# A two-layer hybrid backbone: loads of the opening in another order, one-stretch inputs for the last layer's FFN, and another order of the mLSTM's small matmuls

## Chip, cores and metric

The kernel runs on one core of a Trainium2 chip. The metric is the device time of one execution in microseconds. TensorE (PE) multiplies, VectorE (DVE), ScalarE (ACT) and GpSimd (POOL) do elementwise work, and SyncE (SP) issues all DMA loads in one queue.

## The reference

512 latent tokens and 256 context tokens of width 1024 pass through two layers. A layer has an adaLN-modulated RMSNorm, one input projection for four head groups (A windowed attention, B dense attention with RMS-normalised and rotated q and k, C a bidirectional mLSTM, D a Mamba-2 scan), an output projection of all four, and a squared-ReLU MLP of width 4096. Only the latent tokens leave the kernel. Cut to what the change touches:

```python
def rmsnorm(x, g):
    y = xf * lax.rsqrt(jnp.mean(xf * xf, axis=-1, keepdims=True) + EPS)
    return y * g
# dense attention (B)
q = apply_axial_rope(rmsnorm(q, g_q), cos, sin) * scale
k = apply_axial_rope(rmsnorm(k, g_k), cos, sin)
# mLSTM (C), one chunk
s = einsum('bthd,bshd->btsh', qc, kc) * w
num = einsum('btsh,bshv->bthv', s, vc) + decay_prior * einsum('bthd,bhvd->bthv', qc, c_mat)
den = s.sum(axis=2) + decay_prior * einsum('bthd,bhd->bth', qc, n_vec)
c_new = carry_decay * c_mat + einsum('bsh,bshv,bshd->bhvd', wk, vc, kc)
# MLP
def sq_relu_ffn(h, w1, w2):
    return jnp.square(jax.nn.relu(h @ w1)) @ w2
```

## The kernel before

Activations lie with features on the partitions and tokens along the free axis: context in columns 0 to 255 (CTX), latent tokens in 256 to 767 (LAT). Every large product is done in three matmuls on split operands: a weight or activation is split into a rounded part (`h`, `wh`) and a remainder (`hl`, `wl`); `wh` by `h`, `wh` by `hl` and `wl` by `h` are added in PSUM. `wload` (L167) loads a weight block, rounds it on ScalarE (`wh`) and takes the difference on VectorE (`wl`). The tile framework settles the order of instructions on each engine from the program's order and the data they need; each engine then works strictly in that order.

**Opening (L125 to L150, L523 to L592).** The input x comes in four loads of 768 KB (`xr`, L133). Between them stand the loads of `cc` (the conditioning vectors), `cst` (identity and masks), and `pcol`, `prow` (column and row tables, L128). ScalarE squares x (`sq`), TensorE sums over features (`mx`), ScalarE copies the sums (`ssr`), and after a transpose VectorE computes the reciprocal root (`rj`). TensorE spreads it to a row in PSUM (`prow_`), ScalarE copies it to SBUF (`rowx`). `cond(q)` calls `ada_first` (L227) twice: it loads two 512 KB blocks of conditioning weights (`adaw`), multiplies them by the conditioning vector (`silw`), and writes scale and shift into `mod`. `stage(q, sl)` (L561) normalises two feature chunks (`xn`, then `h`, `hl`), which are multiplied with the first projection weights (`wopen`).

**Fill.** `Stream` (L399) holds a list of small pieces of projection work; `fill(t)` emits pieces until a credit of about t microseconds is used up, so that TensorE has projections between the steps of a scan or an attention. `g_feat` (L444) is such a piece: one block of 128 output features over 8 chunks of 128 input features. `g_do` wraps a short function as a piece.

**mLSTM (L1179 to L1394).** While it runs, the stream holds the output gate and the keys and queries of group B. After each of those projections `norm_b` squares it (`bsq`), `col_b` (L1148) sums the squares in matmuls of 2 columns against `cst`, `rsq_b` (L1158) takes the root on VectorE, and `apply_k` (L1167) spreads it by transposes of `kR`. The state loop (L1215) multiplies, for two directions, `vw` by `ktok` and adds into `SC`. The chunk loop (L1340) then has per block of 128 tokens: `c_raw` (q by k on 64 rows, `s<-qT,kT`), the decay matrix `MB` (load, masks on GpSimd, exponentials on ScalarE, product with `c_raw` on VectorE), `fill`, `inter` (`s<-SC,qT`, 130 columns), `fill`, `num` (`s<-v,MB`, eight matmuls of 65 columns) and an evacuation on VectorE (`den`, `yc`). `c_raw`, `inter` and `num` share two PSUM buffers (`s2`) in turn.

**FFN of the last layer (L1458 to L1559).** `ffn1(b)` computes one eighth of the hidden layer, `ffn2(b)` its part of the output. The norm's row is not yet in the inputs: `h2` holds x times its scale in two halves of 256 columns, with 2 columns of the shift between them. So a group of the first product has two stretches, 258 and 256 columns (`psegs`, L1459), and the evacuation multiplies by the row (`rowt`), adds the shift's part (`bs`) in the ReLU, squares and splits:

```python
V.tensor_copy(bs, o[:, 0, NX:NE])
tt(rv, pp, rw, ALU.mult)
act(r[:, sl], r[:, sl], AF.Relu, bias=bs[:, v:v + 1])
tt(r[:, sl], r[:, sl], r[:, sl], ALU.mult)
split_act(r[:, sl], ah, al, sl)
```

The kernel's order is `ffn1(0)`, `ffn1(1)`, `ffn2(0)`, `ffn1(2)`, `ffn2(1)` and so on.

## Time and profile before

| what | value |
|---|---|
| median of 3 timed runs | 1825.8 us (1821.95 to 1827.46) |
| profiled execution | 1831.02 us, its span 1829.2 us |
| mean granted TensorE clock | 0.981 |
| DMA | 178.85 MB, mean 98 GB/s |
| 301.7 to 399.4 us, layer 0's mLSTM | PE busy 94.53 of 97.70 us, clock 0.88 |
| 1295.4 to 1364.0 us, layer 1's mLSTM | PE busy 63.09 of 68.60 us, clock 0.95 |
| DVE busy over the span | 1167.8 us (64%) |

In the profile, a group is named by line, engine, operation and by the tiles it writes and reads; PEld is the load of a matmul's weights, which runs beside the matmuls. PEclk is the clock that was granted to TensorE as a share of full speed. In windows of the profile the columns are: the window and its length, then busy time and instructions of PE, PEld, DVE, ACT and POOL, the granted clock, the share of the DMA engines, and GB/s. An fp32 matmul shows as two instructions there.

### The profile page before, as it was taken

The numbers are of one execution on the slowest core, as the hardware profiler recorded it, in microseconds if no ns is written. First come the engines' busy times: TensorE is split into PE (matmuls) and PEld (weight loads), VectorE is DVE, ScalarE is ACT, GpSimd is POOL, SyncE is SP. The second block draws the span as 40 slices with busy tenths as digits, with TensorE's granted clock in tenths as the row PEclk, the third lists the DMA queues.
The fourth block names the chain that finished last, engine by engine and source line by source line (L and its number), as shares of the span: only waits on it lengthen the run. The fifth ranks groups of instructions, "written<-read, shape, count | busy, mean of one in ns | idle before, by whom it ended". The sixth has DMA issues, their size and how long they took to land. (4 is left out here: it accounts for less than half of the span.)

```text
span 1829.2 us, 31114 instructions
## 1 busy us (share of the span) xinstructions
PE 1756.3 (96%) x11754; PEld 1541.2 (84%) x11754; DVE 1167.8 (64%) x2601; ACT 896.5 (49%) x1988; POOL 330.4 (18%) x332
## 2 busy tenths in 40 slices
PE   7999999989999999999999999999989999999997
PEld 4898888878788888888888888888868899999997
DVE  3578564587877466465465576875588865555555
ACT  4655635455666464354354446563466643333334
POOL 1200111220023363142242531012020200000001
PEclk8999999889999999999999999999999999999999
DMA  9323443331023243233343422132212132322231
GB/s 336 89 82 110 147 139 95 91 121 41 24 82 112 96 132 103 95 127 98 99 127 98 139 70 61 47 94 93 70 58 70 35 105 92 93 93 93 94 96 65
DMA packets 97685, 178.85 MB, mean 98 GB/s; under 512 B 10624, under 2 KB 19200, under 8 KB 97536
## 3 DMA queue, kind: packets, MB, share of 16 engines
q1 hardware_dynamic: 97536, 176.88, 30.1%
q8 instruction: 92, 1.51, 0.3%
q14 instruction: 57, 0.47, 0.1%
HBM read 172.51 MB, written 4.33 MB: 97 GB/s over the span
## 5 line engine op out<-in xcount | busy, mean ns | idle before, releaser
L104 ACT ACTIVATE wh<-wraw 128x512 fp32r<-128x512 f32 (+1 forms) x392 | 238.4, 618 | 257.1 <-PE bulk L96 136.4
L107 DVE TENSOR_TENSOR wl<-wraw,wh 128x512 fp32r<-128x512 f32 (+1 forms) x392 | 281.9, 725 | 116.9 <-ACT wh L104 108.6
L96 PE MATMUL s<-h,wh 128*128 128x258 f32 (+2 forms) x1040 | 316.2, 313 | 1.1 <-ACT pr L104 1.1
L96 PE MATMUL s<-hl,wh 128*128 128x258 f32 (+2 forms) x1040 | 306.2, 313 | 0.0
L96 PE MATMUL s<-h,wl 128*128 128x258 f32 (+2 forms) x1040 | 252.5, 313 | 0.0
L96 PE MATMUL bulk<-ah,wh 128*128 128x512 f32 (+1 forms) x576 | 218.0, 378 | 3.9 <-DVE mod L107 3.2
L302 POOL TENSOR_TENSOR acc<-acc,adap 128x512 f32<-128x512 f32 x96 | 143.2, 1496 | 412.1 <-ACT acc L104 390.6
L96 PE MATMUL bulk<-ah,wl 128*128 128x512 f32 (+1 forms) x576 | 216.1, 375 | 0.0
L96 PE MATMUL bulk<-al,wh 128*128 128x512 f32 (+1 forms) x576 | 215.9, 375 | 0.0
L96 PEld LDWEIGHTS s<-h,wh 128*128 128x128 f32 x1040 | 197.0, 189 | 22.4 <-ACT pr L104 1.6
L115 DVE SCALAR_TENSOR_TENSOR x<-bulk,mod,x 128x512 f32<-128x512 f32 (+1 forms) x224 | 149.4, 671 | 103.3 <-PE bulk L96 102.2
L96 PEld LDWEIGHTS s<-hl,wh 128*128 128x128 f32 x1040 | 197.5, 190 | 11.8 <-issue 0.4
L96 PEld LDWEIGHTS s<-h,wl 128*128 128x128 f32 x1040 | 166.1, 190 | 1.1
L96 PE MATMUL bulk<-h,wh 128*128 128x512 f32 (+1 forms) x416 | 154.0, 370 | 3.8 <-DVE VS L107 2.3
L96 PE MATMUL bulk<-hl,wh 128*128 128x512 f32 (+1 forms) x416 | 144.8, 348 | 0.0
L96 PE MATMUL bulk<-h,wl 128*128 128x512 f32 (+1 forms) x416 | 144.5, 347 | 0.0
L96 PEld LDWEIGHTS bulk<-ah,wh 128*128 128x128 f32 x576 | 108.3, 188 | 24.9 <-DVE mod L107 4.9
L96 PEld LDWEIGHTS bulk<-ah,wl 128*128 128x128 f32 x576 | 108.2, 188 | 21.2
L96 PEld LDWEIGHTS bulk<-al,wh 128*128 128x128 f32 x576 | 108.3, 188 | 19.4
L104 ACT ACTIVATE relu<-relu,bs 128x512 f32<-128x512 f32 x96 | 58.8, 644 | 131.1 <-DVE relu L107 131.1
L104 ACT ACTIVATE adap<-adar,silw 128x256 f32<-128x256 f32 x192 | 85.2, 497 | 56.9 <-DMA adar<-in_wada_dram 52.6
L107 DVE TENSOR_TENSOR relu<-relu 128x512 f32<-128x512 f32 x96 | 88.1, 943 | 31.4 <-ACT relu L104 31.3
(357 smaller groups left out, 3767.3 us busy)
## 6 DMA issues: line engine op xcount, KB each, us to landing
wraw<-in_wf_dram SPq DMA_DIRECT2D x256, 256.0 KB, 2.7
adar<-in_wada_dram SPq DMA_DIRECT2D x96, 256.0 KB, 3.0
wraw<-in_win_dram SPq DMA_DIRECT2D x80, 256.0 KB, 2.8
ada<-in_wada_dram SPq DMA_DIRECT2D x64, 256.0 KB, 4.0
adaw<-in_wada_dram SPq DMA_DIRECT2D x16, 512.0 KB, 6.8
wraw<-in_wout_dram SPq DMA_DIRECT2D x32, 256.0 KB, 3.0
x<-in_xin_dram SPq DMA_DIRECT2D x8, 768.0 KB, 5.0
CB<-drows SPq DMA_DIRECT2D x10, 512.0 KB, 7.0
```

The source lines that it names most:

```text
L96: return TE.matmul(o, lhsT=l, rhs=r, start=start, stop=stop)
L104: return S.activation(o, i, f, scale=scale, **kw)
L107: return V.tensor_tensor(o, a, b, op)
L115: return V.scalar_tensor_tensor(o, a, s, b, op0, op1)
L302: G.tensor_tensor(acc[:, v], acc[:, v], dst, ALU.add)
```

## The change

1. Opening: all four loads of x (and `cc`) stand first in SyncE's queue, then `cst` and layer 0's `pcol`, then the first four conditioning loads (`ada_load`), then the first weights (`W0`), and only then both `prow` and layer 1's `pcol`. `stage(0)` reads the norm's row from PSUM (`prows`); the copy to `rowx` comes after it.
2. `g_feat` takes a waiting function from the list `mids` and runs it in the middle of its eight chunks. `later` puts `col_b` and `rsq_b` on that list, so the 2-column matmuls fall inside the next projection.
3. State loop: both directions' `vw` are made first, then one `fill` of double size, then all `ktok` matmuls.
4. Chunk loop: `inter` comes straight after `c_raw`; the fills ahead of `num` are put together, and a share (0.4 of `wb`) is put between the two halves of `num`.
5. Last layer's FFN: `whole()` multiplies x by the row on GpSimd, applies scale and shift on ScalarE and splits the result into 512 adjacent columns of `h2`. The upper 256 columns are written before `ffn1(1)`, the lower 256 (over the old inputs) before `ffn1(2)`. From b = 2 on, a group is one stretch of 512 columns, and its evacuation is ReLU, square and split.

```diff
     for q in range(4):
         SY.dma_start(xr[q], xin[:, 2 * q:2 * q + 2, :])
         if q == 0:
             SY.dma_start(cc, cin)
-        if q == 1:
-            SY.dma_start(cs, cst)
-        if q == 2:
-            load_cols(0)
+    SY.dma_start(cs, cst)
+    SY.dma_start(pcs[0], pcol[0])
...
+            todo = mids.pop(0) if mids else None
             for k in range(len(W)):
+                if todo is not None and k == len(W) // 2:
+                    todo()
...
+            raws0 = [ada_load(i, (4, 0)[i]) for i in range(2)]
...
-            cond(0)
-            load_cols(1)
+            cond(0, raws0)
+            W0 = wload([wopen[i, 0] for i in range(2)])
+            for l_ in range(DEPTH):
+                load_row(l_)
+            SY.dma_start(pcs[1], pcol[1])
...
-                    norm_chunk(xr[c // 2][:, c % 2, sl], sl, s[:, c:c + 1], md[:, i, c:c + 1], rows[i], *hs[c], pool=c % 2 == 1)
+                    norm_chunk(xr[c // 2][:, c % 2, sl], sl, s[:, c:c + 1], md[:, i, c:c + 1], (rows if q else prows)[i], *hs[c], pool=c % 2 == 1)
+                if q == 0:
+                    act(rows[i], prows[i], AF.Copy)
...
+        def later(*fs):
+            return g_do(lambda: mids.append(lambda: [f() for f in fs]), 0.4 * len(fs))
...
+        def cq(m):
+            return later(*[col_b(f"q{m}", sl, sqq) for sl in segs_q], rsq_b(f"q{m}", jq))
+
+        gs = [later(*[col_b("k", sl, sqk) for sl in (LAT, CTX)], rsq_b("k")), gq(0, LAT)]
+        gs += [gq(0, CTX)] if need else []
+        gs += [cq(0), g_do(apply_k(LAT), 0.5), g_do(apply_k(CTX), 0.5), gq(1, LAT)]
...
-                fill(wu * fC_)
+                vws.append(vw)
+            fill(2 * wu * fC_)
+            for d in range(2):
+                j, vw = ORDERS[d][st], vws[d]
...
             raw = c_raw(j)
+            inter = s2()
+            for e in range(2):
+                for q in range(2):
+                    er = slice(64 * e, 64 * e + 64)
+                    mm(inter[:, e, q * 130:(q + 1) * 130], qT[er, q, js], SC[er, :, j, q, :])
...
+            fill((wa + 0.6 * wb) * fC_ if ji < nout - 1 else 1.5 * FILL_CB[l][4])
             num = s2()
             for e in range(2):
+                if e:
+                    fill(0.4 * wb * fC_ if ji < nout - 1 else 0.5 * FILL_CB[l][4])
...
+        def whole():
+            for c in range(8):
+                t = T((P, NL), F32, "ada", 4, "xn") if c % 2 == 0 else ta((P, NL), name="xn")
+                nrm.append(t)
+                G.tensor_tensor(t, xr[c // 2][:, c % 2, LAT], rowt[0], ALU.mult)
+                act(t, t, AF.Identity, scale=sc2[0][:, c:c + 1], bias=md[:, 0, 24 + c:25 + c])
+                put_whole(c, 1)
+
+        def put_whole(c, i):
+            dst = slice(NE + 256 * i, NE + 256 * i + 256)
+            split_act(nrm[c][:, 256 * i:256 * i + 256], h2[c][0][:, dst], h2[c][1][:, dst], slice(0, 256))
...
+                    if full:
+                        act(r[:, LAT], o[:, 0, :], AF.Relu)
+                        tt(r[:, LAT], r[:, LAT], r[:, LAT], ALU.mult)
+                        split_act(r[:, LAT], ah, al, LAT)
+                        continue
```

How the change moves instructions is shown at three places. The first is SyncE's queue at the program's start, before:

```order
L133 DMA x_65<-in_xin_dram 128x1536
L135 DMA cc_64<-in_cin_dram 128x16
L133 DMA x_66<-in_xin_dram 128x1536
L137 DMA cst_63<-in_cst_dram 128x386
L133 DMA x_67<-in_xin_dram 128x1536
L129 DMA pcol_69<-in_pcol_dram 128x102
L130 DMA prow_71<-in_prow_dram 128x40
L133 DMA x_68<-in_xin_dram 128x1536
L232 DMA adaw_189<-in_wada_dram 128x1024
```

The same place after the change:

```order
L132 DMA x_65<-in_xin_dram 128x1536
L134 DMA cc_64<-in_cin_dram 128x16
L132 DMA x_66<-in_xin_dram 128x1536
L132 DMA x_67<-in_xin_dram 128x1536
L132 DMA x_68<-in_xin_dram 128x1536
L135 DMA cst_63<-in_cst_dram 128x386
L136 DMA pcol_69<-in_pcol_dram 128x102
L228 DMA adaw_101<-in_wada_dram 128x1024
```

The last quarter of x (x_68) has moved ahead of `cst`, `pcol` and `prow`, and `prow` is gone from this part of the queue.

The second place is TensorE in layer 0's mLSTM, where the first block's `num` ends and the second block begins (`s_...` are the PSUM tiles of the chunk loop, `bulk_...` those of the projections), before:

```order
L96 MATMUL s_792_4147<-v_576_2808,MB_4061 128x65 x8
L96 MATMUL bulk_4141<-cst_63,bsq_4095 128x2 x4
L96 MATMUL s_797_4172<-qT_3419,kT_3082 128x128 x4
L96 MATMUL bulk_4194<-cst_63,bsq_4130 128x2 x2
L221 MATMUL bulk_4198<-cst_63,adrow_3988 128x128
L96 MATMUL s_804_4222<-SC_3795,qT_3419 128x130 x4
L96 MATMUL s_809_4258<-v_576_2808,MB_4177 128x65 x2
```

After the change, the same 2-column matmuls and what stands around them, one block later:

```order
L96 MATMUL bulk_4217<-h_179,wl_4010 128x512
L96 MATMUL bulk_4235<-cst_63,bsq_4095 128x2 x4
L96 MATMUL bulk_4217<-h_181,wh_4015 128x512
L96 MATMUL bulk_4217<-hl_182,wh_4015 128x512
L96 MATMUL bulk_4241<-cst_63,bsq_4143 128x2 x2
L96 MATMUL bulk_4217<-h_181,wl_4016 128x512
L96 MATMUL s_804_4227<-v_576_2808,MB_4200 128x65 x4
L96 MATMUL s_814_4280<-qT_3419,kT_3082 128x128 x4
L96 MATMUL bulk_4217<-h_183,wh_4015 128x512
L96 MATMUL s_815_4285<-SC_3795,qT_3419 128x130 x4
```

The `bsq` matmuls now lie between 512-column projections, `num` comes in halves of four, and `inter` (SC) follows `c_raw` (qT, kT) closely.

The third place is TensorE a few blocks on, where the keys of group B are scaled (`kR`), before:

```order
L96 MATMUL s_825_4372<-v_576_2808,MB_4288 128x65 x2
L96 MATMUL s_830_4397<-qT_3419,kT_3082 128x128
L1176 MATMUL bulk_4366<-cst_63,kR_4364 128x128 x4
L96 MATMUL s_830_4397<-qT_3419,kT_3082 128x128 x3
L1176 MATMUL bulk_4429<-cst_63,kR_4427 128x128 x2
L96 MATMUL s_839_4440<-SC_3795,qT_3419 128x130
L96 MATMUL bulk_4433<-h_168,wh_4001 128x512
```

After the change:

```order
L96 MATMUL s_820_4345<-v_576_2808,MB_4290 128x65 x4
L96 MATMUL s_826_4379<-qT_3419,kT_3082 128x128 x4
L96 MATMUL s_827_4384<-SC_3795,qT_3419 128x130 x4
L96 MATMUL s_838_4441<-v_576_2808,MB_4389 128x65 x4
L1190 MATMUL bulk_4416<-cst_63,kR_4414 128x128 x4
L96 MATMUL s_838_4441<-v_576_2808,MB_4389 128x65 x4
L1190 MATMUL bulk_4424<-cst_63,kR_4422 128x128 x2
L96 MATMUL bulk_4428<-h_173,wh_4003 128x512
```

Here a whole block (`c_raw`, `inter` and `num`) stands between two projections with no projection matmul inside.

More of the change, by code (lines that the diff above doesn't have):

```diff
@@ L225, in ada_cols, with ada_load, ada_first @@
            pcs[l][:, C_BADA + 2 * cb:C_BADA + 2 * cb + 2].unsqueeze(1).to_broadcast([P, 2, 2]), ALU.add)
-    def ada_first(i, cb):
+    def ada_load(i, cb):
+        raws = []
+        for kh in range(2):
+            raws.append(k6(raw_roles[(2 * i + kh) % 8], (P, 4, 256), name="adaw"))
+            SY.dma_start(raws[kh], wada[0, cb, kh])
+        return raws
+    def ada_first(raws, cb):
         pt_ = mx((P, 256))
@@ L442, in tile_hybrid_backbone @@
     fill = stream.fill
+    mids = []
     def g_feat(m, acts, sl, evac):
@@ L569, in tile_hybrid_backbone @@
                     stage(q, sl)
-                W = wload([wopen[i, q] for i in range(2)])
+                W = wload([wopen[i, q] for i in range(2)]) if q else W0
                 WT, WF = W[:2], W[2:]
@@ L1216, in tile_hybrid_backbone @@
             kv_ = mx((P, 2, 2, 65))
+            vws = []
             for d in range(2):
@@ L1352, in tile_hybrid_backbone @@
             tt(MBe, MBe, raw[:, :, 0:256].unsqueeze(1).to_broadcast([P, 2, 2, 256]), ALU.mult)
-            fill(wa * fC_ if ji < nout - 1 else FILL_CB[l][4])
-            inter = s2()
-            for e in range(2):
-                for q in range(2):
-                    er = slice(64 * e, 64 * e + 64)
-                    mm(inter[:, e, q * 130:(q + 1) * 130], qT[er, q, js], SC[er, :, j, q, :])
-            fill(wb * fC_ if ji < nout - 1 else FILL_CB[l][4])
+            fill((wa + 0.6 * wb) * fC_ if ji < nout - 1 else 1.5 * FILL_CB[l][4])
             num = s2()
             for e in range(2):
+                if e:
+                    fill(0.4 * wb * fC_ if ji < nout - 1 else 0.5 * FILL_CB[l][4])
                 for q in range(2):
@@ L1409, in tile_hybrid_backbone @@
                 [(kv, j) for j in out_tok for kv in range(2)]
+        assert not mids
         head = attend_s("B", *units[0])
@@ L1459, in tile_hybrid_backbone @@
         psegs = [(0, slice(NE, NE + NL)), (1, slice(0, NE))] if need else [(0, slice(0, NE)), (1, slice(NE, NE + 256))]
+        def whole():
[8 more added lines that the diff above has]
+            split_act(nrm[c][:, 256 * i:256 * i + 256], h2[c][0][:, dst], h2[c][1][:, dst], slice(0, 256))
+        nrm = []
         def ffn1(b):
+            full = not need and b >= 2
             rl = AT_ROLES[b % 2]
@@ L1469, in ffn1 @@
                 ks = [(m, [i], k) for i in range(2) for m in range(2) for k in range(8)] if b == 0 else [(m, [0, 1], k) for m in range(2) for k in range(8)]
+                sg = [(0, slice(NE, NE + NL))] if full else psegs
+                if full:
+                    ks = [(m, [0], k) for m in range(2) for k in range(8)]
                 for m, pi, k in ks:
@@ L1476, in ffn1 @@
                     h, lo = W[k]
-                    parts = [(o[:, psegs[i][0], 0:psegs[i][1].stop - psegs[i][1].start], psegs[i][1]) for i in pi]
+                    parts = [(o[:, sg[i][0], 0:sg[i][1].stop - sg[i][1].start], sg[i][1]) for i in pi]
                     for pp, sl in parts:
@@ L1482, in ffn1 @@
                         mm(pp, lo[:, ms], h2[k][0][:, sl], False, k == 7)
-                    if k < 7 or pi[-1] == 0:
+                    if k < 7 or (pi[-1] == 0 and not full):
                         continue
@@ L1553, in tile_hybrid_backbone @@
         for b in range(8):
+            if not need and b == 1:
+                whole()
+            if not need and b == 2:
+                for c in range(8):
+                    put_whole(c, 0)
             at = ffn1(b)
```

31 lines of the change are left out of this document (11 added, 20 removed).

## Prediction

> **What bounds the kernel now.** I read the page first: the share of each engine and the granted clock in 40 slices.
>
> ```profile
> PE 1756.3 (96%) x11754; PEld 1541.2 (84%) x11754; DVE 1167.8 (64%) x2601; ACT 896.5 (49%) x1988; POOL 330.4 (18%) x332
> PEclk8999999889999999999999999999999999999999
> ```
>
> TensorE is busy 96% of the span and everything else has slack, so a time is gained in three ways only: TensorE starts earlier, streams fewer or cheaper columns, or runs less at a lowered clock. The second row says that the clock is lower in two places, the opening and slices 15 and 16 (around 320 to 410 us). Next I read windows of those places, then the timeline inside them, then the stage with the most matmuls, the last layer's FFN.
>
> **The opening.** SyncE issues loads in program order. The rows below are windows of the DMA rate, then the timelines of SyncE, ScalarE, VectorE and TensorE (start, duration, engine, what; in brackets the idle time and its releaser).
>
> ```profile
> 5.00:8.60 3.60, 2.47 (x11) 0.59 (x12) 0.85 (x5) 3.03 (x5) 0.00 (x0) 1.00 1.00 405
> 8.60:11.00 2.40, 2.40 (x12) 0.38 (x8) 0.25 (x2) 1.58 (x3) 0.00 (x0) 1.00 0.51 165
> 15.00:25.00 10.00, 8.19 (x75) 4.59 (x79) 2.25 (x14) 2.58 (x6) 0.00 (x0) 0.66 1.04 403
> ...
> 3.82 0.46 SPq L130 DMA_DIRECT2D prow<-in_prow_dram  x1
> 4.32 0.45 SPq L133 DMA_DIRECT2D x<-in_xin_dram  x1
> ...
> 7.25 1.58 ACT L104 ACTIVATE sq<-x 128x768 f32<-128x768 f32 x2 [0.43 <-DMA x<-in_xin_dram]
> 9.65 1.58 ACT L104 ACTIVATE sq<-x 128x768 f32<-128x768 f32 x2 [0.82 <-DMA x<-in_xin_dram]
> 14.43 1.57 ACT L104 ACTIVATE sq<-x 128x768 f32<-128x768 f32 x2 [1.73 <-DMA x<-in_xin_dram]
> 18.02 0.98 ACT L104 ACTIVATE ssr<-mx 64x512 f32<-64x512 f32 x2 [2.02 <-PE mx L96]
> 24.67 0.87 ACT L104 ACTIVATE rowx<-s 128x512 f32<-128x512 f32 x2 [2.29 <-PE s L96]
> 27.29 0.72 ACT L104 ACTIVATE h<-xn,mod 128x512 fp32r<-128x512 f32 x1 [0.28 <-DVE mod L107]
> ...
> 12.49 0.17 DVE L111 TENSOR_SCALAR nsk<-prow 128x4 f32<-128x4 f32 x1 [2.14 <-DMA prow<-in_prow_dram]
> ...
> 28.06 0.39 PE L96 MATMUL s<-wh,h 128*128 128x256 f32 x1 [1.71 <-ACT h L104]
> ```
>
> The second quarter of x lands at 7.25, the third at 9.65, the fourth only at 14.43: between them the queue works on the column and row tables (prow lands at 12.49) and the DMA rate falls from 405 to 165 GB/s. The sum of squares, the statistics' row and the first real matmul at 28.06 all follow that fourth quarter.
>
> The change loads all of x ahead of the tables. Third quarter: the 193 KB of constants (0.48 us at 405 GB/s) no longer stand before it, 9.65 - 0.48 = 9.2. Fourth: one quarter takes 9.65 - 7.25 - 0.48 = 1.9 us, so it lands at 11.1, **3.3 us earlier**. The rest of the chain (ssr, transposes, VectorE's rsqrt, the row's matmuls) is unchanged and moves with it. What could be late next is the conditioning weights: ahead of the first two stand 0.25 MB of tables (0.6 us), perhaps the slow stretch of 8.60:11.00 again (2.40 x (1 - 165/405) = 1.4 us), and their own 1 MB (2.6 us): 11.1 + 4.6 = 15.7, before their matmuls can start at about 16.8. The first weights follow by about 20 us, and are wanted at about 22. The 0.87 us of rowx goes behind h, but h waits for mod, not for rowx, so I count nothing there. **Opening: -3.2 us**; at least -0.6 (if the slow stretch stays ahead of x and only the constants go), at most -4.5 (with rowx and a clock that stays up).
>
> **The last layer's FFN.** Before, 512 tokens run as two stretches of 258 and 256 columns. I take the rate from VectorE's first evacuation of each group, then look at who could do the new work.
>
> ```profile
> 1526.51 0.68 DVE L107 TENSOR_TENSOR relu<-s,row 128x512 f32<-128x512 f32 x1
> 1543.87 0.68 DVE L107 TENSOR_TENSOR relu<-s,row 128x512 f32<-128x512 f32 x1
> 1571.96 0.68 DVE L107 TENSOR_TENSOR relu<-s,row 128x512 f32<-128x512 f32 x1
> ...
> 1461.00:1800.00 339.00, 339.00 (x2196) 309.50 (x2195) 188.46 (x310) 119.51 (x195) 0.00 (x0) 1.00 0.29 92
> ...
> L302 POOL TENSOR_TENSOR acc<-acc,adap 128x512 f32<-128x512 f32 x96 | 143.2, 1496 | 412.1 <-ACT acc L104 390.6 <-ACT adap L104 18.6
> ...
> 1461.08 0.39 ACT L104 ACTIVATE row<-mx 128x256 f32<-128x256 f32 x1 [4.46 <-PE mx L96]
> 1473.03 0.63 ACT L104 ACTIVATE wh<-wraw 128x512 fp32r<-128x512 f32 x1 [5.74 <-PE s L96]
> ```
>
> TensorE is full throughout at full clock. 1526.51 to 1543.87 is three groups of 48 small matmuls, 5.79 us a group. To 1571.96 comes one more group and a block of the second product, 96 matmuls of 512 columns: 28.09 - 5.79 = 22.30, or 0.232 us each. After the change a group is 24 of those, 5.58 us: 0.21 us less, in 6 blocks x 4 groups: **-5.1 us**. VectorE's product with the row and the shift's columns go too, but beside a full TensorE that is worth nothing.
>
> The price is the new inputs: 8 GpSimd products (1.5 us each by the L302 row, so done 12 us after row, at about 1473.5), then on ScalarE 8 affine steps and 8 casts, on VectorE 8 differences. ScalarE has a hole of 5.74 us ending at 1473.03, and the new steps fill it; but the last two affine steps wait for GpSimd and stand ahead of the weights' cast of 1473.03. That cast comes some 2 us later (1473.5 and the last affine step and casts behind it): +2 if TensorE wants these weights at once, 0 if it is still at work on the block before. I take the middle, **+1.0 us** (0 to +3, which is two GpSimd products). The second half of the inputs is written under the 22.30 us of the second product, which covers 8 casts and 8 differences; uncovered, they would cost at most 8 x 0.63 = 5.0 us, by the cast's row at twice their width. FFN: -4.1.
>
> **The mLSTM's stretch, and the clock.** These windows show where the clock falls, then what TensorE does in one of them, and what VectorE does behind it.
>
> ```profile
> 329.40:332.80 3.40, 3.04 (x32) 2.62 (x31) 3.28 (x11) 0.75 (x2) 1.76 (x2) 1.00 0.50 117
> 332.80:336.20 3.40, 3.40 (x38) 2.62 (x38) 2.18 (x7) 0.98 (x4) 2.04 (x3) 0.50 0.60 202
> 349.90:360.10 10.20, 10.20 (x39) 7.60 (x38) 5.72 (x14) 3.56 (x12) 2.85 (x4) 0.50 0.21 52
> 373.80:384.00 10.20, 9.60 (x58) 7.32 (x58) 8.78 (x31) 6.19 (x13) 1.50 (x1) 0.50 0.79 252
> 1336.30:1339.70 3.40, 3.40 (x10) 2.72 (x10) 2.86 (x9) 1.51 (x4) 1.81 (x2) 0.51 0.00 0
> ...
> 329.19 1.00 PE L96 MATMUL bulk<-cst,bsq 128*128 128x2 f32 x8
> 330.12 0.71 PE L96 MATMUL s<-qT,kT 64*128 64x128 f32 x8
> 330.76 0.61 PE L96 MATMUL bulk<-cst,bsq 128*128 128x2 f32 x4
> 331.23 0.31 PE L221 MATMUL bulk<-cst,adrow 128*128 128x128 f32 x1
> 331.47 0.72 PE L96 MATMUL s<-SC,qT 64*128 64x130 f32 x8
> 332.55 0.63 PE L96 MATMUL s<-v,MB 128*128 128x65 f32 x3 [0.36 <-DVE kck L1155]
> ...
> 341.50 0.68 DVE L107 TENSOR_TENSOR yc<-yc,s 128x512 f32<-128x512 f32 x1
> 342.17 1.21 DVE L107 TENSOR_TENSOR MB<-MB,s 128x1024 f32<-128x1024 f32 x1
> ```
>
> Clock 0.50 starts right behind windows with many small matmuls. In 329.40:332.80 TensorE waits 0.36 us in all, yet streams little: eight matmuls of 2 columns take 1.00 us, where a 512-column one takes 0.23, and the window holds no projection at all. Half clock holds for 3.4, 10.2 and 10.2 us in layer 0 and 3.4 in layer 1, 27.2 us, with TensorE busy in nearly all of it: work of 13.6 us takes 27.2, **13.6 us lost**.
>
> The change moves the 2-column matmuls into the middle of the next projection, splits the 65-column ones (MB) by projection matmuls, and joins the two products on 64 rows. In the new order layer 0's first and last low windows and layer 1's are broken up so. But at the key's rotation (kR) MB, qT, SC, MB and kR now stand in a row with no projection among them: I keep two windows of 3.4 us there. **Clock: -(27.2 - 6.8)/2 = -10.2 us** (0 to -13.6).
>
> The Trainium skill, "TensorE: Matmul & The Clock Gate", section "Why this matters for your kernels", lays the drop to idle gaps over about 3 us between bursts. This trace differs: it drops with a longest gap of 0.36 us. By that rule this term is 0; that is a rival below.
>
> What it adds: SC's product (inter) now follows qT's at once, in a PSUM buffer that the turn before frees with yc (0.68 us) right after its MB matmuls. Behind it in TensorE's queue stand projection matmuls that were ahead of it. With VectorE free, 0.68 + 0.16 - 0.71 of qT is under 0.3 us a turn; with an MB product in front (1.21 us) 1.5. Ten turns at 0.4, and once at kR the whole of yc and MB's product, 1.5: **+5.5 us** (0 to +18.9, which is ten times 0.68 + 1.21).
>
> The state update's matmuls (vw) now run for both directions at once:
>
> ```profile
> 301.46 0.28 PE L96 MATMUL bulk<-wh,hl 128*128 128x256 f32 x1
> 301.68 0.45 PE L96 MATMUL mx<-vw,ktok 128*64 128x65 f32 x8
> 302.06 0.38 PE L96 MATMUL bulk<-wh,h 128*128 128x256 f32 x1
> 302.28 0.28 PE L96 MATMUL bulk<-wl,h 128*128 128x256 f32 x1
> 302.40 0.28 PE L96 MATMUL bulk<-wh,hl 128*128 128x256 f32 x1
> ```
>
> A 256-column matmul starts 0.12 us behind its neighbour, but 0.22 on the way into and out of the small ones: 0.2 us an excursion, and 10 of 20 go: **-2.0** (0 to -2.0). The projection matmuls that stand ahead of each pair cover VectorE's vw; without them a pair would wait for one vw more.
>
> **Sum**: -3.2 - 4.1 - 10.2 + 5.5 - 2.0 = **-14.0 us**. The profiled execution took 1831.0 (span 1829.2 and 1.8 around it): 1817.0. It lies 5.2 over the median of the runs shown, 1825.8, so I forecast **1812.0**.
>
> **Rivals.** (1) *The clock does not follow the small matmuls' places*: the windows stay at half clock, and only the rest counts: -14.0 + 10.2 = -3.8, 1822.0. For it: the time at half clock may come from dependencies that move along. Against: the window ahead of 332.80 held nothing but small matmuls. (2) *All clusters dissolve and VectorE keeps up*: -13.6 for -10.2, +2 for +5.5: -20.9, 1804.9. For it: VectorE is busy 64% of the span only. (3) *Slower: inter's early place stalls TensorE in every turn*, since it stands in order behind yc and MB's product: 10 x 1.89 = +18.9, and these stalls keep the clock where it is: -3.2 - 4.1 - 2.0 + 18.9 = +9.6, 1835.4. It decides from 0.93 us a turn with no gain of clock. Against: no such wait shows before, and there projections stood ahead of inter. (4) *The opening does not do what it says*: the slow stretch comes from the queue and not from prow, -0.6 for -3.2: 1814.4.
>
> The Trainium skill, same page, section "What's actually happening", has a free-running window of 3413 ns. The half-clock stretches of 3.4 and 10.2 us agree: so where windows fall shifts with the opening, and from run to run.
>
> **How the numbers follow.** Forecast 0.43, rival (1) 0.17, (2) 0.24, (3) 0.06, (4) 0.10. Within 0.3% (1820.3 to 1831.3) is what a measurement of this kernel can hardly tell from no change. Faster: nearly all of the forecast and (4), all of (2), a little of (1): 0.76. Same: most of (1) and a tail: 0.17. Slower: (3) and its surroundings, 0.07. Range: from a little under (2) to a little over (1), 1801 to 1824; it leaves out (3) and the ends where all bounds fall together.
>
> **What would show it.** Opening: the fourth sq at about 11.1, the first wh matmul at about 25. FFN: groups of 5.6 us from block 2 on, no product with row there; a gap of 1 us near 1473 (less the gains). Clock: no 0.50 right after the first turn's MB; one stretch of about 7 us at kR. Waits: TensorE idle before SC under 0.5 us a turn. It is wrong if the clock rows look as before, or if SC is released by yc for over a microsecond each time.

## The result and the profile after

The changed kernel takes 1819.0 us (median of 13 runs, 1815.89 to 1821.77). The kernel before, run beside it, takes 1831.33 us (13 runs, 1821.95 to 1836.26). The ratio is 0.994 with a 95% interval of 0.9925 to 0.9955, so the change gains about 12 us. The forecast was 1812.0 us with a range of 1801 to 1824. The profiled execution took 1820.27 us (span 1818.5), 10.7 less than the one of before.

The page of the changed kernel, busy time of TensorE and the granted clock in 40 slices:

```profile
PE   7999999989999999999999999999989999999997
PEclk9999999899999999999999999999989999999999
```

Before, the first slice and the eighth and ninth (320 to 410 us) showed a lower clock (the prediction names the same times, but calls them slices 15 and 16). Now the eighth does, and the thirtieth (1320 to 1365 us) is new: half clock has become less in layer 0 and has not gone. Where the 10.7 us lie is read from five stretches of the trace. Each runs from one matmul that both kernels have to another: the opening ends at the first `KHL` by `EO`; the mLSTM stretch of layer 0 runs from the first transpose of `kT` to the 33rd `yh` by `wh`, that of layer 1 from the 13th transpose of `kT` to the 241st `KHL` by `EO`; "inputs" runs from the 353rd transpose of `pr` to the 289th `bulk` of `ah` by `wh` and holds `whole()`; "FFN" runs on to the 561st. The rest is the span less these five; no edit of this study touches its code.

| us | opening | mLSTM, layer 0 | mLSTM, layer 1 | inputs | FFN | rest | span |
|---|---|---|---|---|---|---|---|
| before | 88.2 | 118.3 | 90.7 | 66.6 | 312.7 | 1152.7 | 1829.2 |
| after | 83.8 | 113.1 | 86.6 | 70.5 | 308.2 | 1156.3 | 1818.5 |
| difference | -4.4 | -5.2 | -4.1 | +3.9 | -4.5 | +3.6 | -10.7 |

**Opening.** Windows of the DMA rate, then rows of ScalarE and TensorE in the changed kernel:

```profile
8.60:11.00 2.40, 2.40 (x15) 0.56 (x12) 0.00 (x0) 1.82 (x3) 0.00 (x0) 1.00 1.02 402
...
11.08 1.58 ACT L104 ACTIVATE sq<-x 128x768 f32<-128x768 f32 x2 [0.35 <-DMA x<-in_xin_dram]
13.80 0.98 ACT L104 ACTIVATE ssr<-mx 64x512 f32<-64x512 f32 x2 [1.15 <-PE mx L96]
23.14 0.39 PE L96 MATMUL s<-wh,h 128*128 128x256 f32 x1 [2.11 <-ACT h L104]
```

The stretch that ran at 165 GB/s runs at 402, and the last quarter of x is squared from 11.08 on (14.43 before). The first real matmul comes at 23.14, 4.9 earlier than before. Of these, 3.35 come from the load; the sums behind it gain 0.9 more (`ssr` 18.02 to 13.80), since the clock was halved from 15.4 to 22.2 us before and stays full here until 24.6; the last 0.7 lie behind them.

**mLSTM.** The layer-0 stretch before:

```profile
295.20:413.50 118.30, 110.60 (x799) 92.94 (x800) 74.44 (x207) 53.10 (x121) 22.70 (x24) 0.87 0.30 94
```

and after, with windows inside it, then rows of the second sum of the key's norm, of the key's rotation (`kR`) and of the second sum of a query's norm, and TensorE's groups of `inter` and of the column sums over the whole run (busy, mean ns, idle before and its releasers):

```profile
291.80:404.90 113.10, 101.94 (x800) 87.80 (x800) 74.07 (x207) 53.25 (x121) 21.17 (x24) 0.92 0.31 98
331.80:335.20 3.40, 2.05 (x15) 1.57 (x15) 1.66 (x6) 2.58 (x9) 0.98 (x2) 1.00 0.43 165
335.20:342.00 6.80, 6.80 (x31) 5.38 (x30) 3.99 (x17) 0.00 (x0) 0.00 (x0) 0.50 0.40 77
348.83:352.24 3.41, 2.96 (x28) 2.79 (x28) 3.09 (x8) 1.36 (x5) 1.12 (x1) 1.00 0.54 142
352.24:355.66 3.42, 3.28 (x18) 2.54 (x16) 1.38 (x6) 2.16 (x7) 1.93 (x3) 1.00 0.01 2
359.10:362.50 3.40, 3.40 (x20) 2.55 (x19) 2.87 (x11) 0.83 (x2) 0.20 (x1) 0.50 0.02 5
...
334.29 0.61 PE L96 MATMUL bulk<-cst,bsq 128*128 128x2 f32 x4 [1.35 <-DVE kck L1169]
350.92 0.61 PE L1190 MATMUL bulk<-cst,kR 128*128 128x128 f32 x4
357.93 0.61 PE L96 MATMUL bulk<-cst,bsq 128*128 128x2 f32 x4 [0.60 <-DVE kcq L1169]
...
L96 PE MATMUL s<-SC,qT 64*128 64x130 f32 x80 | 8.5, 320 | 1.8 <-DVE yc L107 1.1 <-DVE den L115 0.7
L96 PE MATMUL bulk<-cst,bsq 128*128 128x2 f32 x64 | 8.1, 245 | 2.3 <-DVE kck L1169 1.6 <-DVE kcq L1169 0.6
```

TensorE is busy 8.7 us less and idle 3.5 us more (118.30 - 110.60 = 7.7, then 113.10 - 101.94 = 11.2). The mean clock rises from 0.87 to 0.92: half clock holds for 10.2 us between 330 and 390 instead of 23.8 (a further 6.8 us at the end of the stretch stand in both). `inter` waits 1.8 us in ten turns for VectorE. A wait that was not forecast stands beside it: the second column sum of a pair now waits for VectorE's copy (`kck`, `kcq`), because `bulk` has two PSUM buffers, the projection that is interrupted holds one and the first sum the other. Half clock follows the windows with the two longest of these waits: from 335.2 behind the 1.35 us, and from 359.1 behind the 0.60 us at 357.93. It does not follow the key's rotation: the window 348.83:352.24 holds only small matmuls, `kR` among them, and the one behind it stays at 1.00.

**FFN.** ScalarE's first step for one group and for the group after next; then TensorE, VectorE and GpSimd around the new inputs, and the window behind:

```profile
1520.07 0.60 ACT L104 ACTIVATE relu<-s 128x512 f32<-128x512 f32 x1 [5.19 <-PE s L96]
1531.24 0.60 ACT L104 ACTIVATE relu<-s 128x512 f32<-128x512 f32 x1 [3.14 <-PE s L96]
...
1458.50 0.58 PE L96 MATMUL s<-h,wl 128*128 128x258 f32 x1 [2.29 <-DVE wl L107]
...
1455.03 0.68 DVE L107 TENSOR_TENSOR relu<-s,row 128x512 f32<-128x512 f32 x1
1456.69 1.75 DVE L107 TENSOR_TENSOR wl<-wraw,wh 128x512 fp32r<-128x512 f32 x1
...
1451.46 12.69 POOL L1489 TENSOR_TENSOR xn<-x,row 128x512 f32<-128x512 f32 x8 [3.76 <-ACT row L104]
...
1458.20:1461.60 3.40, 3.10 (x14) 3.10 (x15) 3.40 (x4) 0.56 (x2) 3.40 (x3) 0.50 0.25 82
```

A group takes (1531.24 - 1520.07)/2 = 5.58 us, as forecast. But TensorE stands still for 2.29 us at 1456.2 (the forecast had a gap near 1473) for a weight's remainder (`wl`), which took VectorE 1.75 us instead of 0.69, while GpSimd multiplied; and half clock for 3.4 us follows at once, another 1.7 us.

### The profile page after: what moved, and what is told of

Read it like the earlier page. It is cut to its first block, busy times and chain, and to the rows that moved or that the text cites. A ratio compares the mean times of both kernels' runs of the same rounds, so it can differ in the third digit from the quotient of the medians.

```text
span 1818.5 us, 29949 instructions
## 1 busy us (share of the span) xinstructions
PE 1741.9 (96%) x11178; PEld 1508.9 (83%) x11178; DVE 1162.6 (64%) x2569; ACT 904.2 (50%) x2012; POOL 341.1 (19%) x340
## 4 chain that ended last, share of the span: by engine, by line
PE 78%; DVE 7%; ACT 5%; DMA 4%; issue 3%; POOL 3%; SPq 0%; POOLq 0%; ACTq 0%; DVEq 0%
PE bulk L96 38%; PE s L96 29%; PE mx L96 8%; PE mx L740 2%; DMA MB<-drows 1%; DMA CB<-drows 1%; ACT wh L104 1%; DVE wl L107 1%; ACT qs L104 1%; DMA adar<-in_wada_dram 1%; POOL acc L304 1%; DVE x L115 1%; DMA x<-in_xin_dram 0%; ACT pr L104 0%; DVE yc L107 0%
## 5 line engine op out<-in xcount | busy, mean ns | idle before, releaser
L96 PE MATMUL s<-h,wh 128*128 128x512 f32 (+2 forms) x848 | 292.4, 347 | 1.1 <-ACT pr L104 1.1
L96 PE MATMUL s<-hl,wh 128*128 128x512 f32 (+2 forms) x848 | 282.3, 346 | 0.0
L96 PE MATMUL s<-h,wl 128*128 128x512 f32 (+2 forms) x848 | 252.1, 346 | 2.3 <-DVE wl L107 2.3
L96 PEld LDWEIGHTS s<-h,wh 128*128 128x128 f32 x848 | 161.1, 190 | 30.9 <-ACT pr L104 1.6
L96 PEld LDWEIGHTS s<-hl,wh 128*128 128x128 f32 x848 | 161.4, 190 | 19.8 <-issue 0.2
L96 PEld LDWEIGHTS s<-h,wl 128*128 128x128 f32 x848 | 143.7, 190 | 12.2 <-DVE wl L107 2.5
L107 DVE TENSOR_TENSOR relu<-relu 128x512 f32<-128x512 f32 x96 | 89.3, 956 | 66.9 <-ACT relu L104 66.6
L96 PEld LDWEIGHTS bulk<-ah,wh 128*128 128x128 f32 x576 | 108.3, 188 | 24.6 <-DVE mod L107 4.2
L96 PE MATMUL bulk<-wh,h 128*128 128x256 f32 (+1 forms) x304 | 92.5, 304 | 0.7 <-DVE ra L107 0.4
```

What stands on the lines that cost most here:

```text
L96: return TE.matmul(o, lhsT=l, rhs=r, start=start, stop=stop)
L107: return V.tensor_tensor(o, a, b, op)
```

## The experiments

Twelve kernels were run. The table has their ratio to the kernel before, run beside them, and the stretches of their one profiled execution. e_open to e_vw are the kernel before with one part of the change; the others are the changed kernel with one edit, e_both with two.

| kernel | median us | ratio (95%) | opening | mLSTM 0 | mLSTM 1 | inputs | FFN | rest |
|---|---|---|---|---|---|---|---|---|
| e_open | 1826.01 | 0.9973 (0.9961 to 0.9985) | 83.3 | 118.3 | 91.0 | 66.5 | 312.8 | 1151.6 |
| e_ffn | 1831.80 | 0.9997 (0.9979 to 1.0015) | 89.8 | 118.3 | 90.7 | 69.6 | 308.3 | 1154.4 |
| e_mids | 1829.18 | 0.9991 (0.9977 to 1.0004) | 85.8 | 118.1 | 87.0 | 66.6 | 312.7 | 1155.1 |
| e_inter | 1824.81 | 0.9968 (0.9952 to 0.9984) | 90.2 | 111.2 | 88.1 | 66.6 | 312.8 | 1153.5 |
| e_vw | 1826.73 | 0.9978 (0.9965 to 0.9991) | 85.6 | 110.9 | 88.6 | 66.6 | 312.8 | 1153.6 |
| e_onesum | 1814.40 | 0.9905 (0.9887 to 0.9923) | 83.8 | 111.2 | 85.4 | 70.7 | 308.2 | 1153.7 |
| e_wholevec | 1816.78 | 0.9918 (0.9903 to 0.9934) | 84.7 | 111.2 | 90.3 | 66.7 | 308.2 | 1154.3 |
| e_wholelate | 1816.93 | 0.9916 (0.9900 to 0.9933) | 84.8 | 112.4 | 88.4 | 69.4 | 308.2 | 1151.8 |
| e_nomids | 1813.77 | 0.9909 (0.9892 to 0.9926) | 84.1 | 107.9 | 87.8 | 70.6 | 308.2 | 1152.2 |
| e_interback | 1818.98 | 0.9936 (0.9920 to 0.9952) | 83.9 | 114.0 | 85.7 | 70.6 | 308.2 | 1155.2 |
| e_prowthird | 1818.64 | 0.9931 (0.9911 to 0.9952) | 84.5 | 110.7 | 88.4 | 70.6 | 308.2 | 1152.4 |
| e_both | 1808.19 | 0.9877 (0.9857 to 0.9898) | 83.8 | 109.1 | 85.0 | 66.7 | 308.2 | 1152.3 |

How far a stretch varies without any edit is read from the same table: the unchanged opening lies between 85.6 and 90.2 in five profiles, the changed one between 83.3 and 84.8 in nine; the rest between 1151.6 and 1156.3 in all fourteen, the highest of them in the changed kernel's own profile. The mLSTM stretches of the unchanged code lie at 118.3 and 90.7 to 91.0 in three profiles, those of the changed code at 110.7 to 113.1 and 86.6 to 90.3 in four. So one profile of an edited mLSTM says little about a difference of 2 or 3 us, and ratios that differ by 0.2% have overlapping intervals.

### e_open: the opening alone

```diff
+    SY.dma_start(cs, cst)
+    SY.dma_start(pcs[0], pcol[0])
...
+            W0 = wload([wopen[i, 0] for i in range(2)])
+            for l_ in range(DEPTH):
+                load_row(l_)
```

> The kernel before with the opening's part alone (all of x first, first conditioning weights next, tables later, row read from PSUM). Theory A (the parts add up; x's fourth quarter was held up by the tables): fourth square of x at about 11.1 us, first wh matmul at about 23.1, every later stage 4.3 us earlier than before as the profile of the full change has it at 84 us; time -4 us. Theory B (only the constants' 0.5 us were in x's way, the rest of the gain in the full change comes from elsewhere): -0.6 us, fourth square not before 13.8.

The opening takes 83.3 us and the kernel 0.27% less, about 5 us: theory A. The fourth square starts at 12.03, not at 11.1, because in this execution the second quarter was late already (8.21 instead of 7.27); the quarters follow each other in 1.9 us, as in the changed kernel. No half clock falls into this opening.

### e_ffn: the new inputs alone

```diff
+            full = not need and b >= 2
...
+            if not need and b == 1:
+                whole()
```

> The kernel before with the one-stretch inputs of the last layer's FFN alone. Theory A (the prediction: groups 0.21 us cheaper, 24 of them, less 1.0 for a weight cast that waits): -4.1 us. Theory B (from the profile of the full change: while GpSimd forms its 8 products, VectorE's tensor_tensor takes 1.7 instead of 0.7 us, a weight's remainder comes late, TensorE waits about 2.3 us and may lose another 1.7 at half clock): groups -4.5, price +2.3 to +4: -0.5 to -2.2 us.

The FFN stretch is 4.4 shorter and the stretch of the inputs 3.0 longer; the time is the same as before (0.9997). Theory B: this part gains next to nothing as it stands.

### e_mids: the column sums alone

```diff
+                if todo is not None and k == len(W) // 2:
+                    todo()
```

> The kernel before with the column sums of the q and k norms moved into the middle of the next projection, and nothing else. Theory A (the clock falls behind windows that stream little, and clusters of small matmuls make such windows): half clock in layer 0's mLSTM (23.8 us before between 330 and 385) falls to about 10 us, and 6 us are gained there, less what the sums wait for in their new place: two bulk PSUM buffers, one of them held by the open projection, so the second sum waits for VectorE's copy (kck) of the first, 1.35 and 0.6 us in the full change; net -3 to -5 us in layer 0. Theory B (the clock follows something else, the sums' place does not matter): 20 us or more at half clock remain, net 0 to +2.

Layer 0's stretch is 0.2 us shorter. Half clock holds there for 20.4 us (338 to 348, 379 to 389), and TensorE waits 1.95 us for `kck` at 337.19. That is theory B for layer 0; in layer 1 the stretch is 3.7 shorter. The kernel gains 0.09%, not told from nothing.

### e_inter: the chunk loop alone

```diff
+            inter = s2()
...
+            fill((wa + 0.6 * wb) * fC_ if ji < nout - 1 else 1.5 * FILL_CB[l][4])
```

> The kernel before with the chunk loop's part alone (inter right behind c_raw, fills joined, a share of the fill between the halves of num). Theory A (the full change's profile: inter waits for VectorE's den and yc 0.2 to 0.9 us in some turns, 1.8 us in layer 0 and 1.6 with what stands beside it in layer 1; the split num breaks one cluster): waits of 2 to 4 us added, half clock in layer 0's mLSTM down by one stretch of 3.4 to 6.8 us: -1 to +2 us net. Theory B (the prediction's size): +5.5 of waits, with the clock where it was: +5 us.

The best single part: 7.1 us in layer 0, 2.6 in layer 1, 0.32% of the time. Neither theory had this size. No wait ahead of `inter` is above 0.3 us in either stretch, and two of the three half-clock stretches of layer 0 are shorter or gone (335 to 339 and 356 to 363 are left). The second of these follows the key's rotation, which stands in the first of two windows here:

```profile
352.30:355.70 3.40, 3.29 (x30) 2.82 (x29) 2.59 (x8) 1.81 (x7) 1.27 (x1) 1.00 0.56 133
355.70:359.10 3.40, 3.40 (x18) 3.30 (x18) 1.34 (x7) 2.22 (x6) 1.92 (x3) 0.50 0.08 24
```

TensorE waits 0.11 us in that window (3.40 - 3.29), which holds small matmuls alone.

### e_vw: the state loop's pairs alone

```diff
+            fill(2 * wu * fC_)
+            for d in range(2):
+                j, vw = ORDERS[d][st], vws[d]
```

> The kernel before with the state loop's pairs alone (both vw first, one fill of double size, then all ktok matmuls). Layer 0's mLSTM stretch, from the first transpose of kT to the 33rd yh by wh matmul, took 118.30 us before, 111.24 with the chunk loop's part alone, 113.07 in the full change. Theory A (the prediction: 10 of 20 excursions of 0.2 us go): -1 us in layer 0, -1 us in layer 1, time -2. Theory B (the pairs cost something that explains why the full change gains less there than the chunk loop alone): +0.5 to +2 us in layer 0, time 0 to +2.

From the first transpose of `kT` to the first `inter`, with the same matmuls in between (268 records in both), layer 0 takes 26.39 us instead of 27.95, and layer 1 22.74 instead of 24.48 (216 records): the pairs themselves are worth 3.3 us, not 2.0. But layer 0's stretch is 7.4 us shorter in this profile, and nothing in its chunk loop was touched. TensorE's rows of the first turn (start, duration) and the windows on both sides of 327.40 in this kernel show why:

```profile
326.23 1.00 PE L96 MATMUL bulk<-cst,bsq 128*128 128x2 f32 x8
327.17 0.72 PE L96 MATMUL s<-qT,kT 64*128 64x128 f32 x8
327.81 0.61 PE L96 MATMUL bulk<-cst,bsq 128*128 128x2 f32 x4
328.28 0.31 PE L221 MATMUL bulk<-cst,adrow 128*128 128x128 f32 x1
328.51 0.72 PE L96 MATMUL s<-SC,qT 64*128 64x130 f32 x8
329.60 0.63 PE L96 MATMUL s<-v,MB 128*128 128x65 f32 x4 [0.36 <-DVE kck L1155]
...
324.00:327.40 3.40, 3.40 (x34) 3.38 (x34) 2.00 (x4) 3.14 (x6) 1.98 (x2) 1.00 0.02 5
327.40:330.80 3.40, 3.04 (x49) 2.56 (x51) 3.40 (x15) 0.00 (x0) 0.90 (x1) 1.00 0.75 196
```

This is the very row of small matmuls that stood in the window 329.40:332.80 before, with the same 0.36 us wait at its end, and half clock followed it there. Here the border of two windows, at 327.40 in this execution, runs through its middle, each window has other work beside it, and the clock stays at 1.00. So in this pair of executions the same cluster costs half clock where it fills one window, and nothing where a border cuts it. It is one pair and no rule: in the changed kernel 348.83:352.24 is filled with small matmuls, and the clock stays up. Nor is the 7.4 us typical: the profiled execution, at 1819.85, was the fastest of this kernel's twelve (the next took 1824.78), and by the times the pairs gain 0.22%, some 4 us.

### e_wholevec and e_wholelate: the price of the new inputs

```diff
-                G.tensor_tensor(t, xr[c // 2][:, c % 2, LAT], rowt[0], ALU.mult)
+                tt(t, xr[c // 2][:, c % 2, LAT], rowt[0], ALU.mult)
```

> The changed kernel with the eight products of the new FFN inputs on VectorE instead of GpSimd. Theory A (GpSimd's products slow VectorE's tensor_tensor from 0.7 to 1.7 us, and so a remainder wl comes 2.3 us late): without them VectorE's instructions take 0.7 us throughout, TensorE's gap before s by wl is under 0.5 us and no half clock follows; the stretch from the 353rd pr transpose to the 289th ah by wh matmul takes 66.6 to 67.5 us instead of 70.5, time -3 to -4 against the full change. Theory B (the prediction: ScalarE's affine steps stand ahead of the weight's cast): the steps stay there, the gap stays at 1 to 2 us, 69 or more.

The products and a remainder on VectorE in this kernel:

```profile
1452.67 0.69 DVE L107 TENSOR_TENSOR wl<-wraw,wh 128x512 fp32r<-128x512 f32 x1
1453.27 0.68 DVE L107 TENSOR_TENSOR xn<-x,row 128x512 f32<-128x512 f32 x1
1453.87 0.69 DVE L107 TENSOR_TENSOR wl<-wraw,wh 128x512 fp32r<-128x512 f32 x1
```

The stretch takes 66.7 us, 0.1 more than before the change: theory A. TensorE has no gap behind `whole()` at all, although ScalarE still does all its affine steps. It is the stretch that shows it: 66.5 to 66.7 us in the seven profiles without GpSimd's products, 69.4 to 70.7 in the seven with them. The time (0.9918 against 0.994) points the same way, with overlapping intervals.

```diff
-            if not need and b == 1:
-                whole()
             at = ffn1(b)
+            if not need and b == 1:
+                whole()
```

> The changed kernel with the new FFN inputs written one step later in the program (behind the second block's first product instead of ahead of it). GpSimd's products still start as soon as the row is there. Theory A (VectorE slowed by GpSimd): the first weights stand ahead of the new steps now, but their remainders run beside GpSimd's products all the same: a gap of 0.5 to 1.5 us remains, the stretch takes 67 to 69 us. Theory B (the order on ScalarE alone): no gap, 66.6 to 67 us.

69.4 us, a little above both theories, with gaps of 0.83 and 1.56 us and VectorE again at 1.77 to 1.80 us a step: a later place keeps most of the price (2.8 of 3.9 us) while GpSimd starts as soon as the row is there. The time is as low as that of e_wholevec (0.9916 and 0.9918), which these stretches do not explain: the rest is 4.5 us shorter than in the changed kernel's profile.

### e_onesum and e_nomids: what the column sums' move is worth

```diff
-                kc = bulk((P, nj, 2))
...
+                kc = bulk((P, NJ, 2))
+                for s_ in sl:
+                    sq = sqs.pop(0)
...
+                V.tensor_copy(kcs[n][:, j0:NJ, :], kc[:, j0:NJ, :])
```

> The changed kernel with the column sums of both token stretches in one PSUM buffer and one copy, so that no sum waits for the copy of the one before. Theory A (the sums' place in the open projection costs in layer 0, since the second sum waits 1.35 and 0.60 us for a copy on VectorE, and the window with that wait leads to the half clock of 335.2 to 342.0): both waits go, one or two half-clock windows of 3.4 us less there, layer 0's mLSTM stretch from 113.1 to 109 to 111.5 us, time -2 to -4 against the full change. Theory B (the half clock there comes from the matmuls of MB, qT, SC and kR in a row at the key's rotation, as the prediction had it): the waits go, the half clock stays, 112.5 or more.

The column sums' waits fall from 2.3 to 0.1 us, and layer 0's stretch takes 111.2 us. The same code without this edit took 113.1, 111.2, 112.4 and 110.7 (after, e_wholevec, e_wholelate, e_prowthird), so this single profile does not settle it; the time does more: 0.9905 against 0.994. Another wait grows: `inter` now waits 3.1 us in all, 1.76 of it at 343.75 for VectorE's `den`, and the half clock that is left (344.8 to 351.6) follows that wait.

```diff
-                if todo is not None and k == len(W) // 2:
-                    todo()
...
+        gs += [g_do(col_b("k", sl, sqk), 0.4) for sl in (LAT, CTX)]
```

> The full change without the move of the column sums (they stay in a row behind their projections, as before). Theory A (the sums' new place is worth nothing in layer 0, where alone it gave -0.2 us, and its waits for kck cost 2 us there): layer 0's mLSTM stretch 109 to 112 us (113.1, 111.2 and 112.4 in three profiles with the sums moved), layer 1's 86 to 89; time within 2 us of the full change, rather below. Theory B (the prediction: the sums' move is what dissolves the clusters): half clock there back to 20 us or more, 116 us or more, time +3 to +6.

Leaving the sums where they were gives 107.9 us in layer 0, the shortest of all, and 0.9909. Theory A, and more than it asked: as written, the move costs some 5 us in company with the other parts (0.3% by the times, 0.994 to 0.9909, whose intervals just touch; by the profiles both mLSTM stretches take 195.7 us together, against 199.1 to 201.4 in the four with the change's code). Without it the other four parts gain in company what they gain alone: 0.27 + 0.03 + 0.32 + 0.22 = 0.84%, and 0.91% together. With one buffer (e_onesum) it is about as good as no move (0.9905 and 0.9909).

### e_interback: inter's early place

```diff
-            fill((wa + 0.6 * wb) * fC_ if ji < nout - 1 else 1.5 * FILL_CB[l][4])
+            fill(wa * fC_ if ji < nout - 1 else FILL_CB[l][4])
+            inter = s2()
...
+            fill(0.6 * wb * fC_ if ji < nout - 1 else 0.5 * FILL_CB[l][4])
```

> The full change with inter put back behind the first fill (the fills still shared out, num still split). Theory A (inter's early place costs its waits for den and yc, 1.8 us in layer 0 and some in layer 1, and nothing hangs on it): time -1 to -3 against the full change, no idle time before SC by qT. Theory B (c_raw and inter, both on 64 rows and streaming little, are worth more together, since each group by itself thins another window): half-clock stretches in layer 0's mLSTM up by 3.4 to 10 us, +2 to +5.

The time is that of the full change (0.9936 against 0.994). The waits ahead of `inter` fall from 1.8 to 0.2 us, but 1.23 us appear ahead of `kR`; half clock in layer 0 is as long as with the change. In the full change the early place is worth neither a gain nor a loss. Its waits come only with the moved sums: `inter` waits 0.2 us in all in the two kernels with the early place and the sums where they were (e_inter, e_nomids), and 0.5 to 3.2 us in the six with both.

### e_prowthird: what held up x

```diff
+        if q == 2:
+            load_row(0)
```

> The full change with layer 0's prow loaded ahead of x's fourth quarter (the constants and pcol stay behind x). Theory A (the prediction: the row table's many small pieces are the slow stretch of 165 GB/s): the rate dips below 250 GB/s between 8.6 and 11 us again and the fourth square starts at 12.2 to 12.8 us instead of 11.08; every later step of the opening is 1.2 us later. Theory B (the slow stretch comes from pcol or from where the queue stands): the fourth square at 11.1 to 11.3.

```profile
8.60:11.00 2.40, 2.18 (x9) 0.38 (x8) 0.00 (x0) 2.10 (x4) 0.00 (x0) 1.00 0.68 259
8.24 1.58 ACT L104 ACTIVATE sq<-x 128x768 f32<-128x768 f32 x2 [1.29 <-DMA x<-in_xin_dram]
10.12 1.58 ACT L104 ACTIVATE sq<-x 128x768 f32<-128x768 f32 x2 [0.30 <-DMA x<-in_xin_dram]
13.46 1.58 ACT L104 ACTIVATE sq<-x 128x768 f32<-128x768 f32 x2 [1.66 <-DMA x<-in_xin_dram]
```

The fourth square starts 2.4 us later than in the changed kernel (13.46 against 11.08), but only 1.4 of that is the table's. The third and fourth square are 3.34 us apart here (10.12 to 13.46) and 1.93 there (9.15 to 11.08): the table of 20 KB, spread over 128 partitions in pieces of 160 bytes, costs the quarter behind it 1.4 us, the size that the prediction had for the slow stretch. The other 1.0 us stands already in the second quarter (8.24 instead of 7.27), which was issued ahead of the table, and e_open, with no table there, has it too (8.21). The rate falls to 259 GB/s in this window. That is theory A for the table. It is not the whole of the slow stretch: in the kernel before, with `pcol` and `prow` ahead of the fourth quarter, the two squares are 4.78 us apart (9.65 to 14.43), 2.9 more than in the changed kernel, and no run moved `pcol` alone. The opening ends only 0.7 us later than in the changed kernel, and the time is the same (0.9931 against 0.994). This execution's clock is full from 24.6 to 28.0 us, where the changed kernel's is halved, and that pays back 1.7 us. Whether a later quarter always does so, or this run's windows fell well, stays open.

### e_both: the two repairs at once

The edits of e_onesum and e_wholevec.

> The changed kernel with the column sums in one PSUM buffer and the eight products on VectorE, both at once. Theory A (the two prices lie in different stretches and add): the stretch of the new inputs at 66.7 us, layer 0's mLSTM stretch at 109 to 111.5, time 3.5 to 7 us below the full change, about 1813. Theory B (where the half-clock windows fall is settled by the grid, and the sums' buffer only shifts it): no better than with the products alone, about 1816.5.

Its page, then `inter`'s wait and the first matmuls of the key's rotation (`kR`), and the window at half clock:

```profile
PE 1731.7 (96%) x11178; PEld 1500.6 (83%) x11178; DVE 1156.3 (64%) x2573; ACT 903.8 (50%) x2012; POOL 329.4 (18%) x332
PEclk9999999999999999999999999999999999999999
...
343.82 0.72 PE L96 MATMUL s<-SC,qT 64*128 64x130 f32 x8 [1.78 <-DVE den L115]
345.99 1.06 PE L1192 MATMUL bulk<-cst,kR 128*128 128x128 f32 x4
...
345.90:349.30 3.40, 3.40 (x18) 3.35 (x18) 1.92 (x5) 1.38 (x5) 1.95 (x3) 0.52 0.05 19
```

1808.19 us, 1.2% below the kernel before (0.9857 to 0.9898) and 10.8 us below the changed kernel, more than the 3.5 to 7 expected. The gains of the two edits, 0.35 and 0.22%, add up to nearly the 0.63% measured: theory A. The inputs' stretch is again 66.7 us. No slice is under 0.9, but 3.4 us of half clock are left in layer 0: they follow the window in which `inter` waits 1.78 us for `den`, and `kR` runs when the clock is already halved. The kernel without the sums' move and with the products on VectorE was not run.

## Why the prediction came out as it did

The sign and the range were right; the forecast was 7 us low. One reading was a slip that does not enter the sum: its "eight matmuls of 2 columns" are four, since an fp32 matmul shows as two instructions. By its own steps:

**The base.** Most of the 7 us is here. The sum said 1817.0 for an execution like the profiled one, and 5.2 were taken off because the three runs shown had a median of 1825.8. Over 11 to 35 runs beside each set of experiments the kernel before had medians of 1831.2 to 1832.5: the profiled 1831.0 was the typical one, and three runs with a spread of 5 us were no base. Without this step the forecast is 1817.0 against 1819.0. That this is so near is in part luck, since errors of both signs cancel: by the profiles the inputs cost 2.9 us more than forecast and the rest 3.6, while the mLSTM's three terms, -6.7 together, came to -9.3 and the opening gained 1.2 more.

**Opening, -3.2 forecast, -4.4 in the profile.** The quarter landed where it was put (11.1 forecast, 11.08). The bound of -4.5 "with rowx and a clock that stays up" is what happened: to the statistics' copy, 3.35 from the load and 0.9 from the clock. Averaged over the profiles with and without the edit it is -3.8 (five openings of 87.9, nine of 84.1). In e_prowthird the fourth quarter comes 2.4 us later and the opening ends 0.7 us later, so how much of the gain is the load's own is not settled.

**FFN groups, -5.1 forecast, -4.5 measured.** The group's new length was right; 24 groups gained 0.19 instead of 0.21 each.

**The new inputs, +1.0 forecast (0 to +3), +3.9 measured.** A wrong mechanism: the forecast priced ScalarE's queue. e_wholevec keeps ScalarE's steps and loses the price. What cost is that VectorE's difference takes 1.75 us while GpSimd multiplies, and then a half-clock window. VectorE's product with the row, whose other input lies in PSUM, took 0.68 at the same time (1455.03). The Trainium skill, "SBUF — State Buffer", section "Who interferes with whom", says so: a VectorE instruction with two SBUF inputs contends with a GpSimd instruction that reads SBUF, one with at most one such input, outside the modes that use two ports, does not. The trace agrees with both halves, and the profile of before had the number as the largest value of a group (ns, min/median/max). Of this group's 64 steps on 512 columns, the 49 that ran with GpSimd idle took at most 0.69 us, and seven beside it 1.77 to 1.78; the eight products with the row (`relu<-s,row`) that ran beside GpSimd took 0.68:

```profile
L107 DVE TENSOR_TENSOR al<-relu,ah x96: 411/692/1782, 534.3 to 1774.2; 128x512 fp32r<-128x512 f32 x64, 128x256 fp32r<-128x256 f32 x32
```

**The clock, -10.2 forecast.** Half clock in layer 0 fell by 13.6 us, worth 6.8; in layer 1 it holds for 10.2 us as before, though 3.4 us of that are idle now (the forecast counted one of layer 1's three low windows). The step that failed is "In the new order layer 0's first and last low windows and layer 1's are broken up so", in two ways. The moved column sums, one of the three parts that were to break the windows up, gave 0.2 us in layer 0 alone and cost some 5 in company. And the two windows that the forecast kept at the key's rotation are not there: both low stretches left in layer 0 follow windows in which a sum waits for VectorE's copy (1.35 and 0.60 us), a term that the forecast did not have, and the clock stays up behind the rotation. That the 10.2 us left in layer 0 are near the 6.8 forecast is luck. That small matmuls without a long wait lower the clock held up in two profiles: before (0.36 us of waiting), and in e_inter, where the window 352.30:355.70 holds the key's rotation with 0.11 us of waiting and half clock follows. It is no rule, as 348.83:352.24 of the changed kernel shows. What a window must hold, and what the place of its borders does, stays open.

By single profiles the sums, the chunk loop and the pairs shorten the two mLSTM stretches by 4.0, 9.7 and 9.5 us alone and by 9.3 together, as if they competed for the same windows. The times say otherwise: the pairs' profile was that kernel's fastest run, the chunk loop and the pairs keep their gains in e_nomids, and it is the sums' move that takes back 0.3%.

**inter's wait, +5.5 forecast, 1.8 measured.** A term of the right mechanism and three times too large: VectorE was free in most turns, and with the sums where they were it was free in nearly all (0.2 us). The sums' waits of 2.3 us were missing; waits of 1.8 us, for other instructions, stood ahead of the sums before the change too.

**Pairs, -2.0 forecast, -3.3 measured (in e_vw), beyond the bound of -2.0.** The price of entering and leaving was counted, not that eight instructions of 65 columns take 0.38 us until the next matmul starts, but sixteen 0.62.

**What nothing in the sum stood for: +3.6 in the rest.** The change's own profile has the longest rest of the fourteen; the other thirteen lie between 1151.6 and 1155.2. It goes with the clock: half clock holds in the rest for 31.4 us, before for 17.3 and in the twelve experiments for 18.5 to 27.8. Why this execution has most of it is not shown.

Of the rivals, (1) fell in layer 0, where half clock did go down, and held in layer 1; (3) fell (1.8 us in ten turns, 0.89 in the worst, where 0.93 in every turn was needed); (4) fell at 11.08. Rival (2), -20.9 us with all clusters gone, fell for the changed kernel: 10.2 us of half clock are left in each layer. e_both gains about as much, by two edits that the rival did not have.

## What to carry to other kernels

Before pricing a new GpSimd step, look for VectorE steps with two SBUF inputs that will run beside it, and at the largest duration of their group, not its median. When small matmuls are put inside a larger product, count the PSUM buffers that are open at once: the interrupted product holds one. Where a kernel loses time to half-clock windows, run each part alone and also leave each out of the whole: the sums' move gained next to nothing alone and cost 0.3% in company. Take the base, and what a part is worth, from many runs: three runs put the base 5 us too low, and one profile showed 7.4 us for an edit whose times show some 4.

## What was not expected of the hardware

- GpSimd's product of two 128x512 tiles (1.6 us each) stretches VectorE's steps with two SBUF inputs beside it from 0.69 to 1.75 us, more than twofold, and a 256-column one from 0.42 to 1.5.
- A broadcast load of 20 KB in 160-byte pieces costs the 768 KB load behind it 1.4 us (e_prowthird, one profile).
- The clock can fall behind windows of 3.4 us in which TensorE waits only 0.36 us, or 0.11 in e_inter, if these are filled with small matmuls. It did not when a border cut the cluster (e_vw), nor behind every window so filled (348.83:352.24 of the changed kernel). The Trainium skill, "TensorE: Matmul & The Clock Gate", section "What's actually happening", has the window free-running; the trace agrees, its borders lay 1.7 us past the span's start in the profile of before (counted modulo 3.41) and between 0.0 and 3.3 in the others.
- One program's runs differ in the clock that they are granted: executions of the changed kernel had spans of 1814.1 us at a mean clock of 0.985 and 1819.6 at 0.981. That the borders' place makes this difference is not shown.
